# A hybrid attention and state-space layer on one core: the attention heads' first two token blocks side by side, a shorter pause in the recurrence, and the norm's two rows from ScalarE's queue

## The chip, the cores and the metric

The kernel runs on one core of one Trainium2 chip. The metric is the device time of one execution in microseconds (us). The kernel before took 1604.91 us in the median of three runs (1604.36 to 1609.29). A profiled execution gives the trace from which all durations here are read.

Names used below: PE is TensorE, ACT is ScalarE, DVE is VectorE, POOL is GpSimd, SP is the engine whose queue issues nearly all DMAs.

## The reference

One layer of a decoder trunk, for 1024 tokens of width 1024, in float32. One input projection feeds two token mixers, differential attention and a chunked state-space recurrence (SSD); their outputs are gated, projected and added to the input. Cut to what matters:

```python
h = rms_norm(x, norm_w)
proj = h @ w_in                                    # 1024 x 11296
q, k, v, z_a, xbc, z_s, dt_raw, gate_logits = split(proj)
# branch A: 8 heads, two softmax maps each, causal, per-head norms of q and k
a = softmax(q1 k1) - lam * softmax(q2 k2)
y_a = rms_norm(a @ v, subln_w) * (1 - lambda_init) * silu(z_a)
# branch B: causal conv, then 32 heads in 4 groups, state 128, 8 chunks of 128 tokens
xs, B, C = split(silu(conv(xbc)))
y_s = ssd_chunked(xs, dt, A, B, C, D)              # a scan over the chunks
y_s = gated_group_rms_norm(y_s, z_s, ssd_norm_w)
merged = sigmoid(g_a) * (y_a @ w_proj_attn) + sigmoid(g_s) * (y_s @ w_proj_ssd)
out = x + merged @ w_out
```

## The kernel before

Every large product is made of three matmuls: each operand is split into a high part and a rest, and high by high, high by rest and rest by high are summed in PSUM. The split of a weight is a conversion on ACT (`w<-raw`) and a subtraction on DVE, for some weights on POOL. Nine buffers hold split weights (`NW`), four hold raw ones as they land (`NRAW`). PSUM has eight banks of 128 x 512, and all accumulators, scores and transposes take theirs from this one ring (`trs`).

The program's order is not that of the code. Generators emit instructions, and a planner (`Plan`) keeps a modelled time `pl.t`: it moves between one stream of bulk products (`bulk`) and many small tasks (`pl.spawn`), each due at a modelled time. What it emits first stands first in an engine's queue, and each engine then runs its queue in that order. A change of one generator or one constant can thus move instructions of all engines from that place on.

The stages, with the times that the trace shows for them:

- **Start, 0 to about 37 us.** `start` loads x tile by tile and the first weights. `norm_rows` broadcasts the two rows of `norm_w` (`nwr`, 1 x 512 each) over all partitions by a matmul with a column of ones into `nwb`. `prep_h` squares a tile of x on ACT, makes the factor `rs`, multiplies x by `rs` and `nwb` on DVE, transposes it on PE (`ph`), and `h_evac` splits the result into `hH` and `hL`. Beside that the first z projection (`pmz`) runs, whose last three token blocks are computed side by side.
- **Front projections, to about 580 us.** z, conv, gates and dt. The recurrence begins in this stretch, with `SLOW` (40 us) between two chunks.
- **Heads, about 580 to 1222 us.** `att_proj` makes one head's q, k, v and gate: eight token blocks `t` of 128 tokens, each the sum over eight weights (`kb`), three matmuls each (`pma`, 128 x 512, 24 a block). All eight weights of a head are used by each block and are released one by one in its last block. `att_evac` empties a block's bank on ACT and DVE, `qk_stack` transposes q and k (`pq`), `att_core` and `att_block` make scores (`sc`), softmax, the transposed probabilities (`pa`, copied by ACT into `at`) and `av`. Between these stand the chunks of the recurrence: `ssd_core` starts one at most every `PACE` modelled us, and a chunk (`ssd_chunk`) transposes its x (`px`, copied into `xn`), multiplies B and C (`pc`, `pb`), reads the state (`pO`), makes a new one (`pS`) and transposes its output (`py`).
- **Gates and output products, to 1511 us, then the last product (`po`).**

Of the kernel before, what the change touches and what calls it, by code (L numbers as in the profile page):

```python
# [15 lines left out]
P = 128  # L16
S = 1024
D = 1024
KB = D // P
NT = S // P  # L20
# [11 lines left out]
C_DT = 9216  # L32
C_GATE = 9248
NBIG, NW, NRAW, NMID, NSM = 17, 9, 4, 16, 8
PACE = 21
FRONT, SLOW = 12, 40.0
FRONT_ORDER = "z0 d0 z1 c16 c20 g0 c0 c2 g2 z2 c4 c6 g4 c18 c22 g6 z3 c8 c10 g8 c12 c14 g10"
PLAIN = (("z", 0),)
# [103 lines left out]
def tile_hybrid_layer(ctx: ExitStack, tc: tile.TileContext, x, norm_w, w_in, q_norm_w, k_norm_w,  # L142
                      diff_lambda, subln_w, conv_w, conv_b, dt_bias, a_log, d_skip, ssd_norm_w,
                      w_proj_attn, w_proj_ssd, w_out, out):
    nc = tc.nc
# [25 lines left out]
    pl = Plan()  # L171
    bigs, mids, sms = Slots(NBIG), Slots(NMID), Slots(NSM)
    trs, qlos = Slots(8), Slots(2)
    trs.line = []
    ws, raws = Slots(NW), Slots(NRAW)
    qkm, atm, ytm, smids = Share(mids, 4), Share(mids, 4), Share(mids, 2), Share(mids, 10)
    heads, abb = Share(bigs, 8), Share(bigs, 1)

    def bigt(shape, dt=F32, name="b"):
        return big.tile(shape, dt, tag="b4", name=name)  # L180

    def midt(shape=(P, 512), dt=F32, name="m"):
        return mid.tile(list(shape), dt, tag="b2", name=name)
# [10 lines left out]
    mmt = trt  # L194

    def hpt(name):
        return hpool.tile([P, KB, S], F32R, tag="h", name=name)
# [4 lines left out]
    def mm(o, lhsT, rhs, start, stop, after=0.0, **kw):  # L202
        nc.tensor.matmul(o, lhsT=lhsT, rhs=rhs, start=start, stop=stop, **kw)  # L203
        n, m = rhs.free_size(), lhsT.free_size()
        if rhs.dtype == F32:
            c = max(4 * n / 2400, 0.215)
        else:
            c = max(n / 2400 + lag[0], 0.057 if m <= 64 else 0.107)
        pl.t = max(pl.t, after) + c
# [5 lines left out]
    def pe_done():  # L215
        return pl.t + 0.2
# [40 lines left out]
    def load(o, i, after=0.0):  # L257
        nc.sync.dma_start(out=o, in_=i)
        q = pl.op("Q", 0.48, max(after, pl.t))
        n = o.free_size() * 512 / 360e3 if o.space != bass.MemoryType.DRAM else i.free_size() * 512 / 360e3  # L260
        return pl.op("D", n, q + 0.6) + lag[1]
# [30 lines left out]
    hH, hL = hpt("hH"), hpt("hL")  # L292
# [315 lines left out]
    def w_need(i):  # L608
        while i not in w_at:
            yield pl.t + 0.1  # L610
        while w_at[i] > pl.t:
            yield w_at[i]

    def w_done(i):
        ws.give(w_slot[i], pl.t + 0.1)
        wts.pop(i)

    def wide(i):
        return wts[i][:, 0].rearrange("p f c -> p (f c)"), wts[i][:, 1].rearrange("p f c -> p (f c)")
# [5 lines left out]
    def steps3(o, a, b, first, last, **kw):  # L625
        mm(o, a[0], b[0], first, False, **kw)
        yield
        mm(o, a[0], b[1], False, False, **kw)
        yield
        mm(o, a[1], b[0], False, last, **kw)  # L630
        yield
# [5 lines left out]
    def load_x(t):  # L637
        k = bigs.take()
        xt = bigt([P, D], name=f"x{t}")
        n = 1 if t else 2  # L640
        at = [load(xt[:, i * D // n:(i + 1) * D // n], xv[t * P:(t + 1) * P, i * D // n:(i + 1) * D // n])
              for i in range(n)]
        xts[t] = (xt, k, at)
# [116 lines left out]
    def proj_tok(pm, t, ids, last):  # L760
        hb = lambda kb: (hH[:, kb, t * P:(t + 1) * P], hL[:, kb, t * P:(t + 1) * P])
        for kb in range(KB):
            yield from w_need(ids[kb])
            while (t, kb // 4) not in h_at:
                yield pl.t + 0.1
            while h_at[t, kb // 4] > pl.t:
                yield h_at[t, kb // 4]
            yield from steps3(pm, hb(kb), wide(ids[kb]), kb == 0, kb == KB - 1)
            if last:
                w_done(ids[kb])  # L770
# [26 lines left out]
    def att_proj(h):  # L797
        ids = w_next(KB)
        ks = []
        for _ in range(4):  # L800
            ks.append((yield from pl.get(heads)))
        v = bigt([P, NT, P], name=f"v{h}")
        zg = bigt([P, NT, P], name=f"zg{h}")
        kk = [bigt([P, S], F32R, name=f"kk{h}{m}") for m in range(2)]
        hd[h] = (v, zg, kk, ks)
        lefts[h] = [NT, {}]
        qk = []
        for t in range(NT):
            k = yield from pl.get(trs, first=True)
            pm = mmt(f"pma{h}{t}")  # L810
            yield from proj_tok(pm, t, ids, t == NT - 1)
            if t % 2 == 0:
                km = yield from pl.get(qkm)
                qk.append([midt([P, 2, 256], name=f"qk{h}{t}"), km, 0])
            pl.spawn(att_evac(h, t, pm, k, qk[-1][0][:, t % 2, :], qk[-1]), pe_done())
            if t % 4 == 3:
                pl.spawn(qk_stack(h, t // 4, qk), pl.t + 3.0)
                qk = []

    def att_evac(h, t, pm, k, qn, cell):  # L820
        v, zg = hd[h][0:2]
        at = pe_done()
        t2 = act(qn, pm[:, 0:256], AF.Square, at)
        t1 = act(zg[:, t, :], pm[:, 384:512], AF.Tanh, at, scale=0.5)
        tv = act(v[:, t, :], pm[:, 256:384], AF.Copy, at)
        yield t2
        ss = tin(4, "ss4")
        nc.vector.tensor_reduce(out=ss, in_=qn.rearrange("p (a d) -> p a d", a=4), axis=AX.X, op=ALU.add)  # L828
        t2 = pl.op("V", 0.335, t2)
        rs = tin(4, "rs4")  # L830
        yield max(t1, t2)
        t2 = rsqrt(rs, ss, 64 * EPS, t2)
        t1 = stt(zg[:, t, :], zg[:, t, :], 1.0, pm[:, 384:512], ALU.add, ALU.mult, t1)
        yield t2
        t2 = tt(qn.rearrange("p (a d) -> p a d", a=4), pm[:, 0:256].rearrange("p (a d) -> p a d", a=4),
                rs.unsqueeze(2).to_broadcast([P, 4, 64]), ALU.mult, t2)
        trs.give(k, max(t2, tv))
        cell.append(t2)

    def qk_stack(h, half, qk):  # L840
        v, zg, kk, _ = hd[h]
        lo, hi = slice(0, 64), slice(64, P)
        cs = slice(half * 512, half * 512 + 512)
        while len(qk[0]) < 5 or len(qk[1]) < 5 or "consts" not in ready:
            yield pl.t + 0.2
        yield max(qk[0][3:] + qk[1][3:] + [ready["consts"]])
        kq = yield from pl.get(bigs)
        kz = yield from pl.get(qlos)
        qh, ql = bigt([P, 2, 512], F32R, name=f"qh{h}{half}"), qlo[kz]
        done = []  # L850
        for isk in range(2):
            k = yield from pl.get(trs)
            pt = trt(f"pq{h}{half}{isk}")
            for i in range(4):
                tp(pt[:, i * P:(i + 1) * P], qk[i // 2][0][:, i % 2, isk * P:(isk + 1) * P])
            if isk:
                for c in qk:
                    qkm.give(c[1], pl.t + 0.1)
            at = pe_done()
            yield at  # L860
            t1 = at
            for m, (own, other) in enumerate(((lo, hi), (hi, lo))):
                if isk:
                    t1 = act(kk[m][own, cs], pt[own], AF.Copy, at)
                else:
                    act(qh[own, m], pt[own], AF.Copy, at, scale=wqk_c[own])
                    t1 = act(qh[other, m], pt[own], AF.Copy, at, scale=wqk_c[own])
            yield t1
            for m, (own, other) in enumerate(((lo, hi), (hi, lo))):
                if isk:  # L870
                    t1 = tt(kk[m][other, cs], pt[own], kk[m][own, cs], ALU.subtract, t1 - HOP)
                else:
                    t1 = stt(ql[own, m], pt[own], wqk_c[own], qh[own, m], ALU.mult, ALU.subtract, t1 - HOP)
            done.append(t1)
            trs.give(k, t1)
        pl.spawn(att_core(h, half, (qh, ql, kq, kz)), max(done))
# [525 lines left out]
    def ssd_core(g):  # L1402
# [20 lines left out]
        for c in range(NT):  # L1423
# [4 lines left out]
            pl.spawn(ssd_chunk(g, c, state, abs_))  # L1428
            yield pl.t + (PACE if bigs.avail(3) <= pl.t or 'setup' in ready else SLOW)

# [525 lines left out]
    nwr = [midt([1, 512], name=f"nwr{i}") for i in range(2)]  # L1956
# [4 lines left out]
    def norm_rows(t):  # L1961
        yield t
        for i in range(2):
            mm(nwb[i], one, nwr[i], True, True)
        ready["nwb"] = pe_done()

    def start():
        load_x(0)
        for i in range(2):
            t = load(nwr[i], norm_w[:, i * 512:i * 512 + 512])  # L1970
        pl.spawn(norm_rows(t), t)
        yield from w_loads(0, 4)
        load_x(1)
        pl.spawn(prep_h(0))
        pl.spawn(prep_h(1), pl.t + 0.01)
        pl.spawn(w_splits(), pl.t + 0.02)
        yield from w_loads(4, 8)
        for t in range(2, NT):
            load_x(t)
            pl.spawn(prep_h(t))  # L1980
        while len(h_at) < 2 * NT:
            yield pl.t + 1.0
        for k, b in zip(kn, kb_):
            mids.give(k, pl.t)
            trs.give(b, pl.t)
# [37 lines left out]
```

## Time and profile before

| what | value |
| --- | --- |
| median of three runs | 1604.91 us |
| the profiled execution | 1603.58 us |
| its span, first to last instruction | 1601.6 us |
| mean granted TensorE clock | 0.998 |
| PE busy | 99% |
| DVE, ACT, POOL busy | 70%, 58%, 47% |
| mean DMA traffic | 147 GB/s |

How to read it: the span is the profiled execution without what lies before its first and after its last instruction. The profile calls an engine busy while an instruction of it runs; matmuls overlap, so that a matmul of 128 x 512 is listed with 0.39 us although the next one starts 0.227 us later. An idle time in square brackets behind a row is that of the engine before this instruction, with what ended it. Idle time of PE is what counts here, since PE is busy for nearly the whole span.

### The profile page before, as it was taken

What the parts mean: (1) busy time and instruction counts of PE and PEld (TensorE: products, weight loads), DVE (VectorE), ACT (ScalarE), POOL (GpSimd) and SP (SyncE); (2) the same over time, 40 slices, a digit from 0 to 9 for tenths busy, and PEclk for the clock granted to TensorE, in tenths of its full rate; (3) what the DMA queues carried; (4) which work ended last, traced back from release to release, by engine and by line L of the source; (5) the groups of instructions that cost most, each with busy time, mean ns of one, the idle gap of its engine ahead of it and who ended that gap; (6) DMA issues with size and microseconds to landing.
All of it is one profiled execution on the core that took longest, in us unless ns stands there. A gap on an engine that the chain in (4) does not pass through costs nothing.

```text
span 1601.6 us, 25383 instructions
## 1 busy us (share of the span) xinstructions
PE 1578.4 (99%) x8446; PEld 1341.7 (84%) x8446; DVE 1119.3 (70%) x2049; ACT 925.9 (58%) x2239; POOL 749.5 (47%) x882
## 2 busy tenths in 40 slices
PE   8999999999999999999999999999999999999999
PEld 6898889888988888888878888888888888888887
DVE  7967674878567756777777777777566677898831
ACT  8444455665565556667677777687666655352310
POOL 3554455554645534445574645455656424222000
PEclk9999999999999999999999999999999999999999
DMA  5233354344354451414372423334435479698941
GB/s 181 93 109 86 119 155 124 113 133 151 109 144 139 125 175 50 119 46 143 112 233 86 146 80 119 93 99 139 135 114 189 137 242 312 213 336 256 328 145 67
DMA packets 229670, 236.04 MB, mean 147 GB/s; under 512 B 15255, under 2 KB 167584, under 8 KB 229538
## 3 DMA queue, kind: packets, MB, share of 16 engines
q1 hardware_dynamic: 229538, 234.41, 46.4%
q8 instruction: 67, 1.10, 0.3%
q14 instruction: 65, 0.53, 0.1%
HBM read 163.96 MB, written 70.39 MB: 146 GB/s over the span
## 4 chain that ended last, share of the span: by engine, by line
PE 85%; ACT 6%; POOL 3%; DVE 2%; DMA 2%; issue 1%; SPq 0%; POOLq 0%; DVEq 0%; ACTq 0%
PE pma L203 16%; PE py L203 6%; PE fYc L203 6%; PE po L203 5%; PE px L203 4%; PE pz L203 4%; PE fXc L203 4%; PE fZc L203 4%; PE pO L203 4%; PE av L203 3%; PE sc L203 3%; PE tyz L203 3%; PE fYg L203 3%; PE pg L203 3%; PE txz L203 2%; PE fZg L203 2%
## 5 line engine op out<-in xcount | busy, mean ns | idle before, releaser
L203 PE MATMUL pma<-w,hH 128*128 128x512 f32 x1024 | 344.2, 405 | 1.1 <-POOL w L237 0.5
L203 PEld LDWEIGHTS pma<-w,hH 128*128 128x128 f32 x1024 | 187.6, 189 | 35.3 <-ACT at L229 1.4
L203 PE MATMUL pma<-w,hL 128*128 128x512 f32 x512 | 206.1, 403 | 0.0
L237 POOL TENSOR_TENSOR rawf<-rawf,rawf 128x512 f32<-128x512 f32 x54 | 70.1, 1299 | 114.7 <-issue 41.5
L203 PEld LDWEIGHTS pma<-w,hL 128*128 128x128 f32 x512 | 96.9, 189 | 16.9
L229 ACT ACTIVATE p<-p,nm 128x512 f32<-128x512 f32 (+7 forms) x128 | 98.6, 772 | 14.9 <-DVE nm L903 10.2
L203 PE MATMUL fYc<-ft,wp 128*128 128x512 f32 x432 | 105.0, 390 | 0.0
L229 ACT ACTIVATE w<-raw 128x512 fp32r<-128x512 f32 (+1 forms) x98 | 60.7, 626 | 60.3 <-PE po L203 22.9
L203 PEld LDWEIGHTS fYc<-ft,wp 128*128 128x128 f32 x432 | 80.9, 188 | 16.7
L229 ACT ACTIVATE wp<-rawp 128x512 fp32r<-128x512 f32 x72 | 44.3, 627 | 82.3 <-POOL rawp L237 23.7
L229 ACT ACTIVATE wp<-rawf 128x512 fp32r<-128x512 f32 x108 | 64.8, 625 | 43.7 <-POOL rawf L237 19.1
L237 POOL TENSOR_TENSOR w<-raw,w 128x512 fp32r<-128x512 f32 (+1 forms) x30 | 39.2, 1308 | 94.6 <-ACT w L229 79.6
L203 PEld LDWEIGHTS av<-v,at 128*128 128x128 f32 x576 | 73.5, 193 | 7.4 <-ACT at L229 3.4
L229 ACT ACTIVATE ab<-ab,nac 128x128 f32<-128x128 f32 x256 | 78.4, 393 | 1.1 <-POOL ab L1412 0.9
L903 DVE CUSTOM_DVE_ANT_0 p<-sc,maskb 128x512 f32<-128x512 f32 (+3 forms) x128 | 72.1, 585 | 9.8 <-PE sc L203 9.6
L266 POOL TENSOR_SCALAR rs<-ss 128x4 f32<-128x4 f32 (+1 forms) x71 | 21.2, 298 | 122.0 <-DVE ss L828 101.9
L203 PE MATMUL av<-v,at 128*128 128x128 f32 x576 | 75.3, 277 | 2.9 <-ACT at L229 2.9
L237 POOL TENSOR_TENSOR rawp<-rawp,rawp 128x512 f32<-128x512 f32 x36 | 52.7, 1475 | 52.3 <-DVE wp L237 37.6
L269 POOL TENSOR_TENSOR rs<-rs,mhalf 128x4 f32<-128x4 f32 (+1 forms) x71 | 73.9, 1041 | 5.9
L203 PE MATMUL sc<-kk,qh 128*128 128x512 f32 (+2 forms) x192 | 66.7, 354 | 0.4 <-DVE kk L237 0.4
L237 DVE TENSOR_TENSOR wp<-rawf,wp 128x512 fp32r<-128x512 f32 x72 | 55.9, 790 | 14.1 <-ACT wp L229 14.0
L237 DVE TENSOR_TENSOR w<-raw,w 128x512 fp32r<-128x512 f32 (+1 forms) x68 | 57.3, 852 | 9.5 <-ACT w L229 9.0
(332 smaller groups left out, 4575.3 us busy)
## 6 DMA issues: line engine op xcount, KB each, us to landing
raw<-in_w_in_dram SPq DMA_DIRECT2D x80, 256.0 KB, 3.1
rawf<-in_w_in_dram SPq DMA_DIRECT2D x72, 256.0 KB, 3.7
ab<-act_d SPq DMA_DIRECT2D x32, 512.0 KB, 4.6
cv_d<-cv SPq DMA_DIRECT2D x48, 256.0 KB, 2.3
t_d<-ts SPq DMA_DIRECT2D x24, 512.0 KB, 3.0
xr<-cv_d SPq DMA_DIRECT2D x32, 256.0 KB, 3.6
zc<-z_d SPq DMA_DIRECT2D x32, 256.0 KB, 3.8
ys_d<-xdt SPq DMA_DIRECT2D x32, 256.0 KB, 2.4
```

Of the source, the lines that this page charges most:

```text
L203: nc.tensor.matmul(o, lhsT=lhsT, rhs=rhs, start=start, stop=stop, **kw)
L229: nc.scalar.activation(o, i, f, **kw)
L237: (nc.vector if eng == "V" else nc.gpsimd).tensor_tensor(out=o, in0=a, in1=b, op=op)
L266: nc.gpsimd.tensor_scalar(out=dst, in0=src, scalar1=add, scalar2=None, op0=ALU.add)
L269: nc.gpsimd.tensor_tensor(out=dst, in0=dst, in1=mhalf[:, 0:cols], op=ALU.pow)
L903: nc.vector.tensor_tensor_reduce(out=p[:, j:e], in0=sc[i][:, 0:e - j], in1=maskb[:, S - n + j:S - n + e], scale=-1.0, scalar=nms[i - 1] if ...
```

## The change

Three edits. In `att_proj` the token blocks 0 and 1 of a head are computed side by side: each weight is used by both blocks, on two PSUM banks, before the next weight; blocks 2 to 7 follow one by one as before. `PACE`, the shortest modelled time between two chunks of the recurrence, becomes 19 instead of 21. In `start` the two rows of `norm_w` are issued first and from ScalarE's queue instead of third and fourth from SP's, and the planner takes them as landed at 2.7 us.

```diff
-PACE = 21
+PACE = 19
@@ att_proj
-        for t in range(NT):
-            k = yield from pl.get(trs, first=True)
-            pm = mmt(f"pma{h}{t}")
-            yield from proj_tok(pm, t, ids, t == NT - 1)
-            if t % 2 == 0:
-                km = yield from pl.get(qkm)
-                qk.append([midt([P, 2, 256], name=f"qk{h}{t}"), km, 0])
-            pl.spawn(att_evac(h, t, pm, k, qk[-1][0][:, t % 2, :], qk[-1]), pe_done())
-            if t % 4 == 3:
-                pl.spawn(qk_stack(h, t // 4, qk), pl.t + 3.0)
+        for ts in ((0, 1), (2,), (3,), (4,), (5,), (6,), (7,)):
+            pms = []
+            for t in ts:
+                k = yield from pl.get(trs, first=True)
+                pms.append((mmt(f"pma{h}{t}"), k))
+                if t % 2 == 0:
+                    km = yield from pl.get(qkm)
+                    qk.append([midt([P, 2, 256], name=f"qk{h}{t}"), km, 0])
+            for kb in range(KB):
+                yield from w_need(ids[kb])
+                for t, (pm, k) in zip(ts, pms):
+                    yield from steps3(pm, hblk(kb, t), wide(ids[kb]), kb == 0, kb == KB - 1)
+                    if kb == KB - 1:
+                        pl.spawn(att_evac(h, t, pm, k, qk[-1][0][:, t % 2, :], qk[-1]), pe_done())
+                if ts[0] == NT - 1:
+                    w_done(ids[kb])
+            if ts[-1] % 4 == 3:
+                pl.spawn(qk_stack(h, ts[0] // 4, qk), pl.t + 3.0)
                 qk = []
+
+    def hblk(kb, t):
+        return hH[:, kb, t * P:(t + 1) * P], hL[:, kb, t * P:(t + 1) * P]
@@ start
+        for i in range(2):
+            nc.scalar.dma_start(out=nwr[i], in_=norm_w[:, i * 512:i * 512 + 512])
+        pl.spawn(norm_rows(2.7), 2.7)
         load_x(0)
-        for i in range(2):
-            t = load(nwr[i], norm_w[:, i * 512:i * 512 + 512])
-        pl.spawn(norm_rows(t), t)
```

The order of instructions is the same before and after on all engines from about 37 us to about 590 us of the trace; it differs in the start, and from the first heads on.

VectorE at the very start, first of the kernel before, then of the change. `x0` is the first tile of x, `nwb0` and `nwb1` the broadcast rows, `w0` to `w4` the first split weights, `ph00` and `ph01` the transposed halves of the tile:

```order
L245 SCALAR_TENSOR_TENSOR ss_144<-ss_144,ss_146 128x1
L245 SCALAR_TENSOR_TENSOR x0_128<-x0_128,rs_148,nwb0_122 128x512
L245 SCALAR_TENSOR_TENSOR x0_128<-x0_128,rs_148,nwb1_123 128x512
L237 TENSOR_TENSOR w0_153<-raw0_133,w0_153 128x512
L237 TENSOR_TENSOR w1_158<-raw1_135,w1_158 128x512
L237 TENSOR_TENSOR w2_166<-raw2_137,w2_166 128x512
L237 TENSOR_TENSOR hL_114<-ph00_160,hH_113 128x4x128
L237 TENSOR_TENSOR w3_175<-raw3_139,w3_175 128x512
L237 TENSOR_TENSOR hL_114<-ph01_169,hH_113 128x4x128
```

```order
L245 SCALAR_TENSOR_TENSOR ss_146<-ss_146,ss_148 128x1
L237 TENSOR_TENSOR w0_150<-raw0_133,w0_150 128x512
L245 SCALAR_TENSOR_TENSOR x0_130<-x0_130,rs_152,nwb0_122 128x512
L245 SCALAR_TENSOR_TENSOR x0_130<-x0_130,rs_152,nwb1_123 128x512
L237 TENSOR_TENSOR w1_156<-raw1_135,w1_156 128x512
L237 TENSOR_TENSOR w2_163<-raw2_137,w2_163 128x512
L237 TENSOR_TENSOR w3_171<-raw3_139,w3_171 128x512
L237 TENSOR_TENSOR hL_114<-ph00_166,hH_113 128x4x128
L237 TENSOR_TENSOR hL_114<-ph01_174,hH_113 128x4x128
```

The first weight's subtraction now stands ahead of the two multiplies of x, and the fourth one ahead of both rests of h.

TensorE at the start of head 3, again before and after. `pma30` and `pma31` are the accumulators of the head's blocks 0 and 1, `w55` and `w56` its first weights; `av21`, `px23`, `pO22`, `px24`, `pO23` and `pya22` belong to other tasks:

```order
L203 MATMUL pma30_8697<-w55_7701,hH_113 128x512
L203 MATMUL av21_8699<-v2_7636,at210_8645 128x128 x2
L203 MATMUL pma30_8697<-w55_7701,hH_113 128x512
L203 MATMUL pma30_8697<-w55_7701,hL_114 128x512
L203 MATMUL pma30_8697<-w56_8585,hH_113 128x512 x2
L203 MATMUL pma30_8697<-w56_8585,hL_114 128x512
L212 MATMUL px23_8736<-ident_98,xr23_8665 128x128 x4
L203 MATMUL pma30_8697<-w57_8639,hH_113 128x512
L203 MATMUL pO22_8604<-xdt22_8432,ab22_8433 128x64 x8
```

```order
L203 MATMUL pma30_8853<-w55_7746,hH_113 128x512 x2
L203 MATMUL pma30_8853<-w55_7746,hL_114 128x512
L212 MATMUL px24_8864<-ident_98,xr24_8799 128x128 x4
L203 MATMUL pO23_8734<-xdt23_8595,ab23_8614 128x64 x8
L203 MATMUL pma31_8855<-w55_7746,hH_113 128x512 x2
L212 MATMUL pya22_8894<-ident_98,y22_8796 128x128
L203 MATMUL pma31_8855<-w55_7746,hL_114 128x512
L203 MATMUL pma30_8853<-w56_8757,hH_113 128x512 x2
L203 MATMUL pma30_8853<-w56_8757,hL_114 128x512
```

Six matmuls now stand between the first use of a weight and that of the next, instead of three, and the recurrence is one chunk further on (`px24` instead of `px23`).

ScalarE at the same place, where the last weights of head 3 (`w61`, `w62`) and the first of head 4 (`w63`) are converted. `at230` is the copy of a block of probabilities, `qh21` the scaled copies of q for head 2:

```order
L229 ACTIVATE yt20_8809<-pya20_8810,cols2_109 128x128
L229 ACTIVATE bT23_8667<-pb23_8818 128x128
L229 ACTIVATE ch23_8826<-cT23_8668 128x128
L229 ACTIVATE w62_8833<-raw62_8779 128x512
L229 ACTIVATE w63_8842<-raw63_8792 128x512
L229 ACTIVATE at230_8840<-pa230_8835 128x512
```

```order
L229 ACTIVATE w61_8940<-raw61_8878 128x512
L229 ACTIVATE ch24_8948<-cT24_8802 128x128
L229 ACTIVATE w62_8955<-raw62_8880 128x512
L229 ACTIVATE w63_8966<-raw63_8888 128x512
L229 ACTIVATE qh21_8959<-pq210_8960,cols2_109 64x512 x4
L229 ACTIVATE xn23_8518<-xn23_8518,rsy_8944 128x512
```

Behind the two conversions there stood a copy of probabilities; now the copies of q stand there.

## The prediction

> **What bounds the kernel now.** I read the head of the page first, to see which engine is full, then the stretches by stage, then what TensorE waited for.
>
> ```profile
> span 1601.6 us, 25383 instructions
> PE 1578.4 (99%) x8446; PEld 1341.7 (84%) x8446; DVE 1119.3 (70%) x2049; ACT 925.9 (58%) x2239; POOL 749.5 (47%) x882
> ```
>
> TensorE (PE) is busy for 1578.4 of 1601.6 us. The change neither adds nor removes a matmul, so only the 23.2 us in which PE is idle can be won, and slow matmuls. The next view says where they lie. Columns: stretch, its length, busy us of each engine with its instructions, granted clock, share of the DMA engines, GB/s.
>
> ```profile
> core 0: us, PE busy (x) PEld busy (x) DVE busy (x) ACT busy (x) POOL busy (x), PEclk, DMA share, GB/s
> 0.00:40.00 40.00, 34.15 (x154) 25.02 (x155) 28.41 (x49) 32.95 (x60) 15.76 (x32) 1.00 0.54 181
> 40.00:590.00 550.00, 547.83 (x3014) 473.64 (x3014) 387.75 (x609) 303.50 (x586) 281.17 (x232) 1.00 0.42 127
> 590.00:660.00 70.00, 69.03 (x372) 57.96 (x371) 46.05 (x99) 43.65 (x126) 31.60 (x48) 1.00 0.32 94
> 660.00:980.00 320.00, 309.42 (x1798) 264.33 (x1797) 236.71 (x525) 228.83 (x681) 175.32 (x267) 0.99 0.37 116
> 980.00:1222.00 242.00, 241.45 (x1383) 206.92 (x1382) 165.35 (x384) 168.25 (x508) 144.66 (x223) 1.00 0.38 119
> 1222.00:1511.00 289.00, 289.00 (x1326) 240.56 (x1325) 230.10 (x350) 138.70 (x264) 97.12 (x80) 1.00 0.78 258
> 1511.00:1602.00 91.00, 87.49 (x409) 73.25 (x407) 24.94 (x37) 10.06 (x16) 3.90 (x3) 0.99 0.40 132
> ```
>
> Length less PE busy: 5.9 us in the start, 2.2 in the front projections, 1.0 + 10.6 + 0.6 = 12.1 in the heads, nothing in gates and products, about 3 behind the last matmul. By the order of instructions the change leaves the front projections, from about 37 to 590 us, as they are, and the products have no idle to give. So two places count: **the start and the heads**. What ended PE's waits (total us, times, longest):
>
> ```profile
> PE nwb L203 <- DMA nwr<-in_norm_w_dram: 4.1, 1, 4.1
> PE av L203 <- ACT at L229: 2.9, 1, 2.9
> PE pS L203 <- ACT at L229: 2.1, 1, 2.1
> PE px L212 <- DVE qk L237: 1.9, 1, 1.9
> PE pO L203 <- DVE ab L237: 1.5, 3, 1.0
> PE pma L203 <- POOL w L237: 0.5, 2, 0.4
> ```
>
> The reader is to see two things. PE hardly waits for a head's weights themselves (the last row, 0.5 us), so the two blocks side by side win next to nothing directly. And most of the heads' 12.1 us lies in four single waits, 2.9 + 2.1 + 1.9 + 1.0 = 7.9 us.
>
> **The start.**
>
> ```profile
> 0.78 1.28 ACT L229 ACT_TABLE_LOAD   x1 [0.78 <-PEq L2010]
> 1.71 0.60 SPq L258 DMA_DIRECT2D nwr<-in_norm_w_dram  x2
> 3.41 0.63 ACT L229 ACTIVATE hL<-x 128x512 fp32r<-128x512 f32 x1 [1.34 <-DMA x<-in_x_dram]
> 4.07 3.75 PE L203 MATMUL nwb<-nwr,one 1*128 1x512 f32 x4 [4.07 <-DMA nwr<-in_norm_w_dram]
> 5.93 1.30 ACT L229 ACTIVATE w<-raw 128x512 fp32r<-128x512 f32 x2 [1.16 <-DMA raw<-in_w_in_dram]
> 7.86 0.75 DVE L245 SCALAR_TENSOR_TENSOR x<-x,rs,nwb 128x512 f32<-128x512 f32 x1 [0.88 <-PE nwb L203]
> 8.53 1.89 DVE L237 TENSOR_TENSOR w<-raw,w 128x512 fp32r<-128x512 f32 x3
> 9.23 0.93 SPq L258 DMA_DIRECT2D raw<-in_w_in_dram  x2
> ```
>
> The norm's rows are issued third and fourth on SP's queue at 1.71 and PE starts at 4.07, 2.36 us later. On ScalarE's queue they come first, at about 0.78 where ACT's first instruction stands. With the same 2.36 us PE starts at 3.14: 0.93 earlier. ACT pays two issues, 0.60 us by SP's row, ahead of its table load; ACT idles 1.34 us before the first square, which covers them, and without that cover they would cost 0.6. The broadcast (3.75) then ends at 6.9 and no longer holds the second multiply at 7.86.
>
> What is late next is VectorE: the changed order puts the first weight's subtraction (0.63, a third of the row at 8.53) ahead of the two multiplies. The raw weights are issued up to 0.6 us earlier on SP, so ACT's first conversion can start at 5.3 instead of 5.93; it takes 0.65, the subtraction ends at about 6.6, and the multiplies at 7.35 and 8.1, against 8.61 for the second one now. That is 0.5 us earlier. The subtraction moved ahead also frees the first raw buffer some 2.5 us before 9.16, and the fifth weight on SP (9.23) was waiting for that; the x tiles stand behind it. Bounds for the start: nothing won, if x alone decides, and 2.5 us, if the whole queue slides with that buffer. I take **1.0**, near the 0.93 of the first wait.
>
> **The heads.** The largest wait, with ACT and PE beside each other:
>
> ```profile
> 822.81 0.63 ACT L229 ACTIVATE w<-raw 128x512 fp32r<-128x512 f32 x1 [1.31 <-DMA raw<-in_w_in_dram]
> 824.16 0.63 ACT L229 ACTIVATE w<-raw 128x512 fp32r<-128x512 f32 x1 [0.72 <-DMA raw<-in_w_in_dram]
> 824.69 0.58 ACT L229 ACTIVATE at<-pa 128x512 f32<-128x512 f32 x1
> ...
> 825.33 1.38 PE L203 MATMUL av<-v,at 128*128 128x128 f32 x8 [2.86 <-ACT at L229]
> ...
> 827.78 0.63 PE L203 MATMUL pma<-w,hH 128*128 128x512 f32 x1
> ```
>
> This is the first block of head 3. Its last weights have not landed; ACT, in order, stands before their conversions for 1.31 + 0.72 us, and the copy of the attention probabilities (`at`) stands behind them. PE reaches `av` early because a block of one token tile gives it 24 matmuls. With two blocks side by side it has six matmuls per weight instead of three: up to the seventh weight 42 instead of 21, which at 0.227 us each (row below) is 4.8 us more work that needs no late weight. In the changed order ACT still converts w62 and w63 back to back there, but behind them stand the scaled copies of q, which PE reads only after both blocks; so that wait should go. The 1.0 us wait (at 727.8) and the 1.9 us wait (at 909.9) also lie in a first block, of heads 2 and 4. The 2.1 us wait (695.6) does not.
>
> ```profile
> 36.80 27.91 PE pmz L203 x123
> ...
> L229 ACT ACTIVATE xn<-px x23: 576/598/625, 592.8 to 1089.8; 128x512 f32<-128x512 f32 x23
> ...
> 680.00:700.00 20.00, 17.89 (x106) 15.43 (x105) 14.81 (x29) 13.42 (x35) 7.40 (x12) 0.91 0.23 73
> 820.00:840.00 20.00, 17.14 (x92) 14.13 (x91) 12.54 (x25) 13.44 (x36) 14.63 (x18) 0.91 0.76 246
> 900.00:920.00 20.00, 17.84 (x111) 15.14 (x110) 14.46 (x28) 15.16 (x46) 12.76 (x21) 1.00 0.58 165
> ```
>
> 27.91 / 123 is 0.227 us a matmul, and the last 72 of these 123 are three z blocks side by side: alternating PSUM banks costs nothing here. The last three rows show what a wait costs beside itself: around the waits of 2.9 and 2.1 us the granted clock is 0.91 over 20 us, so 20 x 0.09 = 1.8 us more each, and around 1.9 us it stays 1.00. **The price of a wait over 2 us is therefore itself and 1.8.** All that the heads hold is 12.1 + 3.6 = 15.7 us.
>
> The Trainium skill ("TensorE: Matmul & The Clock Gate", Part 1 and "Why this matters for your kernels") says that the clock halves after an idle window of about 3.4 us and that gaps under about 3 us keep it. The trace differs: 2.1 us were enough. By the page's rule the heads' pool would be 12.1 us.
>
> Of the first-block waits, 2.9 + 1.9 + 1.0 = 5.8 and the 1.8 of clock, 7.6 in all, I let two thirds go, 5.0: one of the three may come back elsewhere, since everything else on ACT and DVE is reordered too. Ends: nothing, and the full pool of 15.7.
>
> The shorter **pause**: 23 chunks lie 497.0 / 22 = 22.6 us apart now; scaled by 19/21 they come every 20.4, and the last chunk some 47 us earlier (less, if tiles hold it back). No work goes. ACT and DVE, busy for 229 and 237 of 320 us (72 and 74%) in the worst stretch, take the chunks' share about a tenth denser. Against harm speaks that between 980 and 1140 chunks still run and the whole row from 980 to 1222 idles only 0.6 us. Ends: 3.9 us won (the 695.6 wait and its clock go) and 3.9 lost (one more such wait); I take 0.5 lost.
>
> **Sum.** 1.0 + 5.0 - 0.5 = 5.5 us. The profiled execution took 1603.6 us (its span and 2.0 around it), the median of the three runs is 1604.9. 1603.6 - 5.5 = 1598.1, and the median lies a little above such an execution: **1598.5**.
>
> **Rivals.**
>
> *The waits only move.* PE runs through a fixed order, and both queues it waits for are reshuffled from 590 us on; a fresh order has its own late moments. For it speaks that the four waits have four different causes, against it that three of them sit at the same place of a head. This holds as well if the rows do not land earlier from ScalarE's queue. Then the pool stays at 15.7 and the start gives 1.0 or nothing: 1602.6 to 1603.6. Chance 0.28.
>
> *Nearly all goes.* The start wins 2 and the heads 10 to 12: about 1591. Chance 0.12.
>
> *PSUM banks become the wait (slower).* All projections, scores, transposes and recurrence steps share eight banks, and a head's start now holds two of them through both blocks instead of one at a time. The wait at 909.9 is of this sort (a transpose waits for `qk`'s multiply to free its bank), and so is the one at 695.6 (`pS` waits for the copy `at`). If the second bank brings one wait of 2.1 us and its 1.8 of clock at a head's start, that is 3.9 a head; with 5.5 won elsewhere it decides from the second head on, and at four of the five heads that share PE with the recurrence it gives 1598.5 + 15.6 = 1614. Against it: the planner places work only where it has a bank, so it would show as another order, not as a wait. Chance 0.13.
>
> *Alternating banks slow PE.* If the 48 matmuls of each pair ran at half clock for half of the time, 24 x 0.227 = 5.4 us a head, the eight heads would cost 44: about 1642. Chance 0.02, since the z blocks run at 0.227. The Trainium skill ("TensorE: Matmul & The Clock Gate", "A second HAM failure mode: psum-queue depth-cycling") describes such oscillation; the `pmz` row does not show it.
>
> **Chances and range.** The forecast has 0.45 and covers 1596 to 1601. A change of 0.3%, 4.8 us, is about what a measurement of this kernel can tell from no change, so faster means below 1600.1: 0.40 of the forecast's 0.45 and the 0.12 make 0.52. Same: 0.05 and 0.28 and 0.01 of the bank rival, 0.34. Slower: 0.14. The range runs from the good rival, 1591, to 1605, past the moved waits; the bank rival stays out.
>
> **What would show it.** Start: the norm's broadcast on PE at 3.0 to 3.3 us and the row of 4.1 in PE's waits at about 3.1; PE's unbroken run beginning at 36 instead of 36.8. Heads: PE idle between 590 and 1222 us down from 12.1 to about 7, no `av` wait behind a landing weight in a first block, and one stretch with a clock of 0.91 instead of two. Pause: the last `xn<-px` before 1065. I am wrong if the idle sum of the heads stays or grows, if new waits name PSUM readers (`qk`, `at`, `v`) at head starts, or if PE idles after 1222, where I count nothing.

## The result, and the profile after

| | before | after |
| --- | --- | --- |
| median, same chip | 1604.63 us (1603.80 to 1609.29, 4 runs) | 1592.42 us (1592.12 to 1594.14, 4 runs) |
| profiled execution | 1603.58 us | 1592.12 us |
| its span | 1601.6 us | 1590.3 us |
| mean granted TensorE clock | 0.998 | 1.000 |

The ratio of the times is 0.9925, with a 95% interval of 0.9911 to 0.994: 12.2 us faster. The forecast was 1598.5 us, 6.4 below the 1604.91 us known then. The sign holds, and 1592.42 lies in the range of 1591 to 1605; it lies below the 1596 to 1601 that the forecast itself covered, and the gain forecast is about half of what came.

The head of the page of the kernel after, and then the first six of the prediction's seven stretches (stretch, length, busy us and instructions of each engine, granted clock, share of the DMA engines, GB/s):

```profile
span 1590.3 us, 25366 instructions
PE 1573.1 (99%) x8446; PEld 1339.3 (84%) x8446; DVE 1121.8 (71%) x2049; ACT 925.2 (58%) x2239; POOL 751.0 (47%) x882
```

```profile
0.00:40.00 40.00, 34.42 (x155) 25.66 (x156) 28.33 (x49) 32.42 (x59) 15.76 (x32) 1.00 0.55 181
40.00:590.00 550.00, 547.86 (x3014) 473.72 (x3013) 383.74 (x605) 303.68 (x585) 280.38 (x230) 1.00 0.42 127
590.00:660.00 70.00, 68.34 (x370) 57.12 (x369) 48.51 (x104) 44.44 (x130) 33.06 (x51) 1.00 0.31 93
660.00:980.00 320.00, 317.27 (x1878) 273.27 (x1877) 250.28 (x550) 239.28 (x715) 185.88 (x280) 1.00 0.39 123
980.00:1222.00 242.00, 240.90 (x1363) 206.16 (x1362) 159.91 (x368) 165.15 (x491) 139.62 (x215) 1.00 0.39 127
1222.00:1511.00 289.00, 288.43 (x1318) 239.71 (x1317) 232.87 (x351) 133.27 (x252) 93.32 (x74) 1.00 0.78 258
```

From 660 to 980 us PE idles 320 - 317.27 = 2.7 us, where it idled 10.6, and 1878 instead of 1798 of its instructions start there. Over the three rows of the heads the idle time is 1.7 + 2.7 + 1.1 = 5.5 us, before 12.1. The start idles 5.6 (before 5.9), the front projections 2.1 (2.2), and gates and products, which had nothing, 0.6.

What ended PE's waits in the kernel after (total us, times, longest):

```profile
PE nwb L203 <- POOL one L1970: 2.7, 1, 2.7
PE ph L212 <- DVE x L245: 2.4, 1, 2.4
PE pma L203 <- POOL w L237: 1.7, 1, 1.7
PE fXg L203 <- ACT fc L229: 1.5, 2, 1.0
PE py L212 <- ACT xn L229: 0.9, 2, 0.4
PE av L203 <- ACT at L229: 0.5, 1, 0.5
```

Of the four waits of before, on `at` (twice), `qk` and `ab`, that made 7.9 us, 0.5 us on `at` is left; the one large wait in the heads is a new one of 1.7 us, on a weight. It is followed by no loss of clock: both stretches that stood at 0.91 are at 1.00 now.

```profile
680.00:700.00 20.00, 19.67 (x117) 16.49 (x116) 13.37 (x27) 15.53 (x43) 5.57 (x12) 1.00 0.24 73
820.00:840.00 20.00, 20.00 (x110) 16.74 (x109) 16.72 (x35) 14.23 (x36) 15.54 (x17) 1.00 0.87 281
```

The start in the order of time (start, length, engine, instruction; in brackets the idle time before it):

```profile
0.79 0.74 ACTq L1980 DMA_DIRECT2D nwr<-in_norm_w_dram  x2
1.56 1.28 ACT L229 ACT_TABLE_LOAD   x1 [1.56 <-PEq L2021]
1.69 1.85 SPq L258 DMA_DIRECT2D raw<-in_w_in_dram  x4
2.74 3.77 PE L203 MATMUL nwb<-nwr,one 1*128 1x512 f32 x4 [2.74 <-POOL one L1970]
6.84 2.60 ACT L229 ACTIVATE w<-raw 128x512 fp32r<-128x512 f32 x4 [1.69 <-DMA raw<-in_w_in_dram]
8.11 1.40 DVE L245 SCALAR_TENSOR_TENSOR x<-x,rs,nwb 128x512 f32<-128x512 f32 x2
8.91 1.97 PE L212 MATMUL ph<-ident,x 128*128 128x128 f32 x8 [2.39 <-DVE x L245]
```

PE's first matmul starts at 2.74, 1.3 us earlier than before. Yet the first weights, issued earlier, are first converted at 6.84 instead of 5.93; the subtraction that now stands ahead of the two multiplies on DVE waits with them, so that the second multiply ends later than before (8.11 + 1.40 = 9.51, before 7.86 + 0.75 = 8.61) and PE waits 2.4 us for it. In the chain of work that ended last, PE's unbroken run of `pmz` begins at 36.51, before at 36.80: 0.3 us are left of the 1.3.

To see where the 11.3 us of span went, I cut both traces at the first matmul of a few tiles. Up to the first `pma`: 579.2 us before, 578.9 after. From there to the first matmul of the gates: 643.2 and 630.7. The gates: 59.9 and 61.3, the products 228.6 and 228.5, and from the first `po` to the end 90.6 and 91.0. In the heads, 12.5 us went; 1.4 of them came back in the gates, where some attention work now stands. Of the 11.1 us net, 6.8 - 0.8 = 6.0 are idle time between the same cuts (12.1 against 5.3 in the heads, 0.8 against nothing behind them), 3.6 are the two losses of clock, and 1.5 are left that neither view shows; gaps too short to stand out behind the modelled ends of matmuls would be one way.

### The profile page after: what moved, and what is told of

It reads as the page before. It is cut to its first block, busy times and chain, and to the rows that moved or that the text cites. A ratio compares the mean times of both kernels' runs of the same rounds, so it can differ in the third digit from the quotient of the medians.

```text
span 1590.3 us, 25366 instructions
## 1 busy us (share of the span) xinstructions
PE 1573.1 (99%) x8446; PEld 1339.3 (84%) x8446; DVE 1121.8 (71%) x2049; ACT 925.2 (58%) x2239; POOL 751.0 (47%) x882
## 4 chain that ended last, share of the span: by engine, by line
PE 90%; ACT 3%; DMA 2%; DVE 2%; POOL 1%; issue 1%; SPq 0%; DVEq 0%; POOLq 0%; ACTq 0%
PE pma L203 19%; PE py L203 6%; PE fYc L203 6%; PE po L203 5%; PE pO L203 4%; PE sc L203 4%; PE pz L203 4%; PE px L203 4%; PE fXc L203 4%; PE av L203 4%; PE fZc L203 4%; PE tyz L203 3%; PE fYg L203 3%; PE txz L203 2%; PE fZg L203 2%; PE pa L212 2%
## 5 line engine op out<-in xcount | busy, mean ns | idle before, releaser
L229 ACT ACTIVATE p<-p,nm 128x256 f32<-128x256 f32 (+7 forms) x128 | 98.9, 776 | 33.5 <-DVE nm L914 27.6
L229 ACT ACTIVATE wp<-rawf 128x512 fp32r<-128x512 f32 x108 | 64.9, 625 | 43.1 <-POOL rawf L237 19.0
L946 POOL TENSOR_TENSOR rec<-s,mone 128x1 f32<-128x1 f32 x64 | 35.8, 562 | 78.0 <-ACT p L229 77.8
```

Source lines behind the costliest of these rows:

```text
L229: nc.scalar.activation(o, i, f, **kw)
L946: nc.gpsimd.tensor_tensor(out=rec, in0=sums[1], in1=mone, op=ALU.pow)
```

## The experiments

The prediction's theory (**T1**): the waits belonged to a head's first block, and the pair removes them, because it gives PE more work before the late weights. The rival (**T2**): any change of the generators gives a fresh order with late moments of its own, and this one was a good draw. A third question was what the pause and the norm's rows do by themselves. Each kernel was timed in three rounds beside runs of the kernel before on the same chip (its medians: 1605.87 us for the first four, 1604.62 for the second four, 1605.19 for the last four).

### One part at a time

Two blocks side by side alone, on the kernel before:

```diff
-        for t in range(NT):
+        for ts in ((0, 1), (2,), (3,), (4,), (5,), (6,), (7,)):
```

> Only the two blocks side by side; the pause stays at 21 and the norm's rows stay on SP's queue. Theory 'relief of the first block': the waits in first blocks of heads (2.9, 1.9 and 1.0 us, and 1.8 us of reduced clock behind the first) go, the wait of 2.1 us in mid-head and its 1.8 us may stay: 6 to 8 us faster than before, about 1597 to 1599. Rival 'every new order draws its own waits': anything from 8 us faster to 4 us slower, with waits over 1 us at other places. Rival 'the shorter pause does it': within 2 us of before.

The pause alone:

```diff
-PACE = 21
+PACE = 19
```

> Only the pause of 19 instead of 21; blocks one by one, norm's rows on SP's queue. Theory 'relief of the first block': within 4 us of before, either way, with waits of PE of 1 to 3 us still in the first blocks of heads 2 to 4. Rival 'the shorter pause does it': 8 to 11 us faster, about 1594 to 1597. Rival 'every new order draws its own waits': anything from 8 us faster to 4 us slower.

The norm's rows alone:

```diff
@@ start
+        for i in range(2):
+            nc.scalar.dma_start(out=nwr[i], in_=norm_w[:, i * 512:i * 512 + 512])
+        pl.spawn(norm_rows(2.7), 2.7)
         load_x(0)
-        for i in range(2):
-            t = load(nwr[i], norm_w[:, i * 512:i * 512 + 512])
-        pl.spawn(norm_rows(t), t)
```

> Only the norm's two rows first and on ScalarE's queue; the order from 37 us on is that of before. From the changed kernel's trace, where PE's unbroken run begins at 36.5 instead of 36.8 us: 0.3 us faster than before, not to be told from no change in the total, and the same four waits in the heads at times 0.3 us earlier. Rival 'a shift in time changes what collides': the waits in the heads differ by more than 2 us in sum though the order is the same.

Both heads' edits without the norm's rows, that is the kernel after with its start undone:

```diff
-PACE = 21
+PACE = 19
-        for t in range(NT):
+        for ts in ((0, 1), (2,), (3,), (4,), (5,), (6,), (7,)):
```

> Blocks side by side and the pause of 19, but the norm's rows on SP's queue: the changed kernel's order from 37 us on with the start of before. If the start is worth 0.3 us, 11.5 to 12 us faster than before, about 1592.7, and no more than 1 us slower than the changed kernel. If the start were worth what was forecast, 1 us slower than the changed kernel.

Measured (ratio to before with its 95% interval; "heads idle" is PE's idle time from the first `pma` to the gates; "heads to `po`" is the time from the first `pma` to the first `po`):

| kernel | median us | ratio | heads idle us | heads to `po` us |
| --- | --- | --- | --- | --- |
| before | 1605.87 | 1 | 12.1 | 931.7 |
| after (timed earlier) | 1592.42 | 0.9925 [0.9911, 0.9940] | 5.3 | 920.5 |
| pair alone | 1610.03 | 1.0026 [1.0015, 1.0037] | 4.8 | 937.9 |
| pause alone | 1605.99 | 1.0007 [0.9997, 1.0016] | 16.2 | 933.8 |
| norm's rows alone | 1603.04 | 0.9984 [0.9975, 0.9993] | 11.9 | 931.9 |
| pair and pause | 1594.64 | 0.9938 [0.9917, 0.9958] | 5.1 | 922.3 |

Pair and pause each bring nothing or a loss, and together they bring about 10 us (0.9938). The norm's rows are apart from that: alone they bring a little, their order differs from that of the kernel before in the start only, and the heads idle as before (11.9). The other row with an order used twice, pair and pause, has that of the kernel after from 37 us on, and takes 922.3 us where the kernel after takes 920.5. So an order keeps its idle time of the heads from trace to trace (11.9 and 12.1, 5.1 and 5.3); each of these numbers is of one traced execution.

With the pair alone the heads are as good as in the kernel after (4.8 us idle), but gates and products, 288.5 us before, take 306.3. PE's waits there, and when SP issued the pairs of half-sums (`ts`) that the products need, in this kernel and then in the kernel after:

```profile
PE py L203 <- DVE u L237: 8.4, 2, 6.1
PE py L203 <- DVE hH L237: 1.9, 1, 1.9
PE py L203 <- DVE hL L237: 1.0, 1, 1.0
```

```profile
1291.70 0.94 SPq L258 DMA_DIRECT2D ts<-ys_d  x2
1318.58 0.82 SPq L258 DMA_DIRECT2D ts<-ya_d  x2
1390.39 0.91 SPq L258 DMA_DIRECT2D ts<-ya_d  x2
```

```profile
1163.71 1.50 SPq L258 DMA_DIRECT2D ts<-ys_d  x2
1187.48 1.29 SPq L258 DMA_DIRECT2D ts<-ya_d  x2
1279.05 0.99 SPq L258 DMA_DIRECT2D ts<-ya_d  x2
```

With the pair alone the last pair of the recurrence's halves (`ys_d`) is fetched at 1291.70, with the pause of 19 as well at 1163.71, inside the heads. The planner gives these loads their buffers only when enough are spare (`spare`), and with the pair alone that was so only after the heads. The whole row of sums then falls into the products, where weights are landing as well. In the windows of this kernel the DMA engines' share is 0.97 and then 0.68 there; PE idles 5.2 us in the first and 6.1 in the second, whose clock is 0.90 (same columns as the stretches above):

```profile
1400.00:1440.00 40.00, 34.78 (x147) 27.81 (x146) 31.23 (x45) 15.80 (x29) 14.45 (x11) 0.98 0.97 333
1440.00:1480.00 40.00, 33.88 (x134) 27.36 (x134) 32.28 (x48) 10.15 (x18) 8.26 (x6) 0.90 0.68 220
```

A pause of 21 doesn't by itself hold the sums back: the kernel before, with the same pause, fetches the last of these pairs at 1171.58 us, inside the heads, and loses nothing behind them.

### Is it the pair, or the order that came out?

The pair with the old pause, but the half-sums let in earlier (the kernel after with two edits):

```diff
-PACE = 19
+PACE = 21
-        return 0 if done else 3
+        return 0 if done else 2
```

> Blocks 0 and 1 side by side, norm's rows first on ScalarE's queue, pause back at 21, and the two buffers of the half-sums handed out when two instead of three others are left (spare() returns 2), so that the sums of the second half of the recurrence and of the attention stand as early as in the changed kernel. Theory 'late sums cost the arm with the pause of 21': no wait of PE over 1 us between 1290 and 1520 us and a time within 3 us of the changed kernel, 1591 to 1596. Rival 'the pause of 19 itself brings the gain': the products still wait or the heads wait more, 1603 to 1609.

The kernel after with a pause in between:

```diff
-PACE = 19
+PACE = 20
```

> The changed kernel with a pause of 20 instead of 19. Theory 'side by side relieves the heads, whatever the pause, as long as the sums come early' (they do in its order): idle of PE from 590 to 1222 us of 4 to 7 us, no stretch there with a reduced clock, 1591 to 1596. Rival 'every new order draws its own waits': idle of 4 to 14 us, up to 1604.

The same pause without the pair (the kernel before with the norm's rows from ScalarE's queue):

```diff
-PACE = 21
+PACE = 20
```

> The kernel before with the pause of 20 and the norm's rows first on ScalarE's queue, blocks one by one. Theory 'side by side relieves the heads': idle of PE in the heads of 10 us or more and at least one stretch of reduced clock, as in the two other orders without the pair (12.1 at 21, about 16 at 19), 1601 to 1606. Rival 'every new order draws its own waits': idle as low as 5 us is as likely, 1593 to 1606.

The kernel after with blocks 2 and 3 side by side instead of the first two:

```diff
-        for ts in ((0, 1), (2,), (3,), (4,), (5,), (6,), (7,)):
+        for ts in ((0,), (1,), (2, 3), (4,), (5,), (6,), (7,)):
```

> The changed kernel with blocks 2 and 3 side by side instead of 0 and 1, everything else as changed. Theory 'the relief is in the first block, where a head's weights arrive': waits of 1 to 3 us in first blocks of heads are back, idle in the heads 9 us or more, 1599 to 1605. Rival 'any pair does it' (longer runs of matmuls without other engines, wherever they lie): 1591 to 1596.

| kernel | median us | ratio | heads idle us | heads to `po` us |
| --- | --- | --- | --- | --- |
| pair, pause 21, sums early | 1594.79 | 0.9935 [0.9920, 0.9950] | 6.8 | 924.5 |
| pair, pause 20 | 1605.86 | 1.0008 [0.9997, 1.0018] | 13.8 | 935.4 |
| no pair, pause 20 | 1594.08 | 0.9931 [0.9916, 0.9946] | 6.1 | 922.5 |
| blocks 2 and 3, pause 19 | 1606.50 | 1.0007 [0.9997, 1.0017] | 13.6 | 933.1 |

The first row shows what the shorter pause did for the pair: with the sums early by another way, no wait of PE stands between 1290 and 1520 us, and the pause of 21 comes within 3 us of the kernel after. In the pair's order the shorter pause let the sums in before the last heads.

The second and third rows decide whether the gain needs the pair. **With** the pair and a pause of 20 nothing is won; **without** the pair and with the same pause the gain of the kernel after is there to within 2 us. First the whole stretch of the heads in the one and in the other, then PE's waits in the one and in the other:

```profile
580.00:1222.00 642.00, 628.21 (x3572) 536.30 (x3571) 450.27 (x1009) 445.14 (x1325) 356.18 (x541) 0.99 0.38 118
880.00:900.00 20.00, 16.91 (x99) 13.77 (x98) 19.06 (x42) 14.99 (x44) 11.80 (x17) 0.91 0.76 230
900.00:920.00 20.00, 14.49 (x91) 12.52 (x91) 14.11 (x29) 17.74 (x52) 9.85 (x18) 0.91 0.09 31
1000.00:1020.00 20.00, 18.07 (x94) 14.91 (x92) 14.44 (x25) 12.77 (x32) 9.40 (x13) 0.91 0.54 153
```

```profile
580.00:1222.00 642.00, 635.88 (x3640) 543.18 (x3640) 456.69 (x1021) 452.29 (x1339) 360.26 (x551) 1.00 0.39 122
```

```profile
PE av L203 <- ACT at L229: 4.1, 2, 3.9
PE py L212 <- ACT xn L229: 3.5, 5, 1.9
PE px L212 <- DVE nm L914: 1.9, 1, 1.9
```

```profile
PE py L212 <- ACT yt L229: 1.0, 1, 1.0
PE pma L203 <- DVE w L237: 0.9, 1, 0.9
PE av L203 <- ACT at L229: 0.7, 1, 0.7
```

With the pair, PE waits 3.9 us for `at` again, and three stretches of 20 us stand at a clock of 0.91. Without the pair no wait of the heads exceeds 1.0 us, although each head begins with a single block. So the pair does not secure the gain, and the gain does not need it. The fourth row, blocks 2 and 3, agrees by its time with T1 (the first blocks single, the waits back) and with T2 (another order).

The 3.9 us are not the kind of wait that the pair was to remove, though. They stand between two heads: from 881.5 to 919.5 us PE has no matmul of a projection, only the small ones of attention and recurrence. The stretch with all its work, then with the instructions of `pma` alone (the one on PE is the end of head 3's last), then ACT and PE at the wait:

```profile
881.50:919.50 38.00, 29.40 (x175) 24.47 (x173) 31.17 (x69) 30.95 (x89) 19.65 (x34) 0.91 0.43 132
881.50:919.50 38.00, 0.16 (x1) 0.00 (x0) 1.37 (x4) 0.70 (x3) 0.91 0.43 132
898.32 2.77 ACT L229 ACTIVATE qh<-pq,cols 64x512 fp32r<-64x512 f32 x4 [3.73 <-PE pq L212]
904.33 3.27 PE L203 MATMUL av<-v,at 128*128 128x128 f32 x16 [3.85 <-ACT at L229]
```

Ahead of the copy `at`, ACT waited 3.7 us for PE's transposes (`pq`) and not for a weight, and the last weight ahead of head 4 was split by 892.2 us. The waits of 1.89 and 1.94 us in the stretches at 880 and 1000 us also stand ahead of a head's first projection (heads 4 and 5). The program takes two banks before a pair's first matmul and one before a single block's; whether that is what held head 4 up is not shown.

### How much does an order alone move?

`HOP` is the modelled delay between two engines, 0.12 us. It is only a number of the planner: 0.01 more or less changes no operation, and every task may move. Four orders, of the kernel after and of the kernel before with the norm's rows from ScalarE's queue:

```diff
-HOP = 0.12
+HOP = 0.11
```

> The changed kernel with one modelled figure of the planner altered by 0.01 us: HOP, what it adds to an operation's end before another engine may use it, is 0.11 instead of 0.12. No work changes, only the order that comes out. Theory 'every new order draws its own waits, the pair and the pause have no effect of their own': idle of PE in the heads anywhere between 5 and 16 us, the total between 1591 and 1607, and the two such runs of the changed kernel no better on average than the two of the kernel without the pair. Rival 'the pair lowers the waits on average': idle of 4 to 8 us here and in the next run.

```diff
-HOP = 0.12
+HOP = 0.13
```

> The changed kernel with HOP at 0.13. As for 0.11: by the theory of the drawn order anything from 1591 to 1607, by the rival idle of 4 to 8 us in the heads and 1590 to 1597.

Without the pair, 0.11 and then 0.13:

```diff
-HOP = 0.12
+HOP = 0.11
```

> The kernel before with the norm's rows first on ScalarE's queue, blocks one by one, pause of 21, and HOP at 0.11. By the theory of the drawn order anything from 1591 to 1607, the same as the runs with the pair on average; by the rival 'the pair lowers the waits on average' idle of 10 us or more in the heads and 1600 to 1607.

```diff
-HOP = 0.12
+HOP = 0.13
```

> As the run before, with HOP at 0.13: by the theory of the drawn order 1591 to 1607, by the rival 1600 to 1607 with 10 us or more of idle in the heads.

| kernel | median us | ratio | heads idle us | heads to `po` us |
| --- | --- | --- | --- | --- |
| pair, pause 19, HOP 0.11 | 1622.54 | 1.0106 [1.0091, 1.0121] | 6.9 | 921.9 |
| pair, pause 19, HOP 0.13 | 1615.08 | 1.0059 [1.0044, 1.0074] | 12.6 | 933.1 |
| no pair, pause 21, HOP 0.11 | 1629.93 | 1.0149 [1.0132, 1.0166] | 10.5 | 927.6 |
| no pair, pause 21, HOP 0.13 | 1613.87 | 1.0054 [1.0039, 1.0069] | 9.7 | 929.6 |

A hundredth of a microsecond in the model costs 11 to 30 us on the chip, against the same two kernels with 0.12 (1592.42 and 1603.04). All four times lie above every range that was expected of them (1607 us at the most). In three of the four all or nearly all of the loss lies in the front projections, whose order all the other kernels share, and in the fourth (pair, 0.13) 12.4 of 22.7 us; the stretch from 37 to 590 us in the kernel after and with HOP 0.11 in it:

```profile
37.00:590.00 553.00, 550.86 (x3027) 476.17 (x3027) 386.11 (x614) 306.65 (x589) 280.38 (x230) 1.00 0.42 126
```

```profile
37.00:590.00 553.00, 536.41 (x2911) 462.10 (x2910) 376.91 (x588) 296.08 (x569) 272.88 (x223) 0.98 0.39 117
```

PE's idle time there is 2.1 us in the one and 16.6 in the other. Three orders of the front were run in all: that of 0.12 idles 2.1 to 2.5 us, that of 0.11 16.6 and 18.8, that of 0.13 10.4 and 10.7. The order that idles 2 us is thus one that a hundredth loses.

For the heads, whose place in time does not matter to their length, these four give more draws. From the first `pma` to the first `po`: with the pair on blocks 0 and 1, six orders took 937.9, 920.5, 924.5, 935.4, 921.9 and 933.1 us, a mean of 928.9. Block by block, five orders took 931.7, 933.8, 922.5, 927.6 and 929.6, a mean of 929.0. The heads' idle time is 8.4 us in the mean with the pair and 10.9 without, from 4.8 to 16.2. The orders differ by 17 us, the two ways by 0.1. (The 937.9 us of the pair alone hold 11.3 us of idle time from its late sums; up to the first matmul of the gates the means are 635.3 and 637.6 us.) By the pause, the means are 930.3 (21, five orders), 929.0 (20, two) and 927.3 (19, four). No order beat the kernel after.

The sum hides where the idle time lies. I went through PE's instructions of each trace and split it: from a head's first `pma` to its 49th (the first two blocks), from its last to the first of the next head (between heads), and the rest, each summed over the eight heads. No run was made for this split; it reads the traces that were there.

| orders | first two blocks, us | between heads, us | rest, us |
| --- | --- | --- | --- |
| pair, six orders | 0.6, 0.7, 1.2, 1.9, 2.0, 3.4; mean 1.6 | 0, 0, 0, 1.9, 4.5, 10.9; mean 2.9 | mean 3.8 |
| block by block, five orders | 3.3, 6.3, 6.4, 6.5, 7.5; mean 6.0 | 0, 0, 0, 0, 1.2; mean 0.2 | mean 4.7 |
| blocks 2 and 3 side by side | 7.3 | 0 | 6.3 |

In its place T1 holds: with the pair the first two blocks idle less at each pause (0.6 and 2.0 against 6.3 to 6.5 at 21, 0.7 against 3.3 at 20, 1.2 to 3.4 against 7.5 at 19), and blocks 2 and 3 side by side do nothing for them. That the cause is the work ahead of late weights is argued; it fits a wait such as this, in the first block of head 3 without the pair (HOP 0.11):

```profile
849.15 0.80 PE L203 MATMUL pma<-w,hH 128*128 128x512 f32 x1 [3.50 <-POOL w L237]
```

In the sum T2 holds: in three of the six orders with the pair PE idles between heads, in one of them for 10.9 us, and the rest of the heads varies as much. The net effect of the pair, some 2 us, is not clear of that spread.

## Why the prediction was right or wrong

**What bounds the kernel.** Right in the main: PE's idle time and its clock make 9.6 of the 11.1 us. PE's busy time fell by 5.3 us (1578.4 to 1573.1) with the same 8446 matmuls, of which the two losses of clock account for 3.6.

**The start, 1.0 us.** Right in size by the traces, wrong in its steps. The broadcast came earlier than forecast, 2.74 instead of 3.0 to 3.3. What ended PE's wait is POOL's column of ones, not the rows, which ScalarE's queue had delivered by then. But the step by which the raw weights are issued up to 0.6 us earlier and ACT's first conversion can start at 5.3 failed: it started at 6.84, the multiplies went late with the subtraction ahead of them, and this pair of traces shows 0.3 us. The size comes from more traces: the first matmul of `dt` (`pdt`) starts at 64.5, 65.0, 65.6 and 64.4 us in four with the old start, at 64.3, 63.9, 63.3, 64.5, 63.8, 63.6, 64.7 and 64.4 in eight with the new one (HOP 0.11 gave the start another order and is left out). The means are 64.9 and 64.1: 0.8 us, with a spread of 1.2 and 1.4. The times of the norm's rows alone give more, 0.16% or 2.6 us, with an interval of 1.1 to 4.0; pair and pause without the rows took 2.2 us more than the kernel after (1594.64 and 1592.42, timed in different sessions).

**The heads, 5.0 us.** They gave about 11 net, of a pool that I had put at 15.7. The pool and the price of its losses of clock were right: 12.1 us idle fell to 5.3, and 3.6 of clock to nothing. The term itself, what the first blocks give, came nearly as forecast: their idle time fell from 6.4 to 3.4 us, and the loss of clock behind the wait at 825 us went, 3.0 + 1.8 = 4.8. (One reading behind it was wrong: the wait at 727.8 us stands ahead of head 2's first projection, in a stretch of 5.5 us between two heads, and not in a first block.) The part that was mis-sized is the one that I put at nothing. The wait of 2.1 us in mid-head went with its loss of clock, and so did the wait between heads: 2.7 + 1.8 + 1.2 = 5.7 us. Nothing in the change aims at those. Orders with the pair idle 1.9 to 6.9 us in the rest of the heads and 0 to 10.9 between them, so this half of the gain is the order that came out, and luck. With a pause of 20 the first blocks idled 0.7 us, less than in the kernel after, and nothing was won at all; that the sign of the forecast held is thus in part luck too.

**The pause, 0.5 lost.** By itself it measures 1.0007, no change, so the term holds for the pause alone. The recurrence ends earlier, as forecast: the last `xn<-px` stands at 1047 us, where 1065 was forecast and the kernel before has 1090. With the pair the pause did something else than the two effects that I weighed: the half-sums get their buffers before the last heads. That goes with some 15 us (1610.03 with the pause of 21, 1594.64 with 19), and I had counted nothing after 1222 us. The kernel with the sums let in another way shows that the late sums cost it, and not the density of the chunks. Since the kernel before has its sums early at a pause of 21, the late sums belong to the order of the pair alone and not to that pause.

**The price of a wait over 2 us, put at itself and 1.8.** The 1.8 holds, the bound doesn't. In the trace of the pair with the pause of 20, matmuls behind a wait of 1.94 us ran slow:

```profile
1003.68 0.66 PE L212 MATMUL py<-ident,xn 128*128 128x128 f32 x4 [1.94 <-ACT xn L229]
1004.95 0.63 PE L203 MATMUL pma<-w,hL 128*128 128x512 f32 x1
```

A `pma` takes 0.63 instead of 0.39 us there, in the stretch from 1000 to 1020 us whose clock is 0.91. With the pause alone, a wait of 2.13 us at 1164 leaves the clock at 1.00 (timeline, then the window around it):

```profile
1164.23 0.33 PE L212 MATMUL pq<-ident,qk 128*128 128x128 f32 x1 [2.13 <-DVE qk L237]
```

```profile
1155.00:1175.00 20.00, 17.87 (x88) 14.62 (x87) 12.76 (x29) 10.51 (x26) 14.14 (x14) 1.00 0.63 209
```

So around 2 us a wait may or may not cost the clock; what PE ran on either side of these waits differed too, and was not sorted out. The Trainium skill ("TensorE: Matmul & The Clock Gate", Part 1) calls the window in which activity is watched free-running; that the same length of wait has both outcomes fits this. Its rule that the clock halves after an idle window of about 3.4 us does not fit: the waits of 1.89 and 1.94 us stand in stretches with a clock of 0.91.

**The rivals.** "The waits only move" had half of the mechanism: a fresh order has its own late moments. Its price was wrong, since I kept the pool at 15.7 us in every order, whereas orders of the same work idle between 4.8 and 16.2 us in the heads. "Nearly all goes" had the size, 1591 us, for a reason that wasn't stated then. "PSUM banks become the wait" did not come in the kernel after: no wait above 0.5 us in its heads names `at` or `qk`. The late start of head 4 with the pair and a pause of 20 may be of its kind, but as another order and not as a wait, as was said against it; this is not shown. "Alternating banks slow PE" did not come either, since PE's busy time fell.

## What to carry to other kernels

Where a planner sets the order, an edit has two effects: what it does by itself, and the fresh order that it draws; the second can be larger by far, and one trace cannot tell them apart. Before an edit is credited with a gain, time it with the other edits undone and under two or three changes that mean nothing (a hundredth in a modelled delay), and compare the spread. Then split the idle time by the place that the edit aims at: here the first blocks show the pair's own effect in eleven orders, and the total does not.

## What was not expected of the hardware

- In the first 8 us, weights that were issued earlier were not there earlier: their loads started at 1.69 us on SP's queue, and the first was converted at 6.84 us, where before it was at 5.93. In all ten traces with the new start it was at 5.81 to 6.84, in the four with the old one at 5.76 to 5.97. The Trainium skill ("DMA: Bandwidth & Descriptors", "Issuing engines are not separate DMA queues") says that another issuing engine saves only the time to issue, since all transfers share the same 16 engines; that agrees with the weights here.
- The small rows do come earlier by being first: in four traces with the rows third and fourth on SP's queue PE's first matmul started at 4.07, 4.52, 4.95 and 4.04 us, with the rows first on ScalarE's queue always at 2.73 or 2.74, where POOL's column of ones is the limit.
- Some orders vary more from run to run than others: the kernel without the pair at a pause of 20 took 1593.58 to 1594.29 us in four runs with a clock of 1.000, the pair at the same pause 1603.73 to 1608.83 in ten with 0.994 to 0.999. A lost clock alone does not make the spread: the pair with HOP 0.11 took 1622.09 to 1622.97 us with 0.991 to 0.993.
